# An output projection with some of its products saved, and the last residual columns turned another way

## The chip, the cores and the metric

The kernel runs on one core of one Trainium2 chip. The metric is the device time of one execution in microseconds, the median of several runs. The engines of a core that matter here are TensorE (PE, matrix products), VectorE (DVE), ScalarE (ACT), GpSimd (POOL, here mostly as an issuer of DMAs) and SyncE (SP, which issues the loads of weights). Each works through its own queue of instructions in an order that is fixed when the kernel is compiled, and waits on semaphores for the others.

## What is computed

One layer of a decoder trunk over 256 tokens with 2048 features, all in float32. Cut to what matters:

```
h = rms_norm(x, mix_norm_g);  z = h @ w_in            # one projection for all mixers
ha = mLSTM heads of z, normed and gated               # 4 heads of 256
hb = forgetting attention heads of z                  # 8 heads of 128
x = x + concat([ha, hb]) @ w_out                      # the output projection, 2048 x 2048
h = rms_norm(x, ffn_norm_g)
a, g = split(h @ w_up)                                # the up stage, 2048 x 11264
x = x + (gelu(causal_dwconv(a)) * g) @ w_down         # the down projection
x = x + sigmoid(rms_norm(x, ple_norm_g) @ w_ple_gate) * (p @ w_ple_proj)
```

## The kernel before

**Products.** A float32 product is made of three matmuls in float32r: every operand is split into a high part (a cast on ScalarE) and the rest (a subtraction on VectorE), and hi*hi, hi*lo and lo*hi are added in PSUM (`three`, lines 355 to 358; `token_group` has the same three in lines 345 to 347). The left operand, activations turned so that features lie on partitions, is kept in tiles of 128 features (a K tile): `hT` for the input projection, `catT` for the output projection, `x2T` for the up stage. A column of such a tile holds the 256 tokens' high part and then their low part. The right operand is a weight tile, loaded from HBM by SP into one of the raw buffers (512 KB for 128 x 1024), split by ScalarE and VectorE into `hi` and `lo` buffers, of which there are four of each, and used by PE. The work is a list of blocks; `run_stream` (line 261) walks through it, loads as far ahead as raw buffers are free and splits up to three blocks ahead (`AHEAD_SPLIT`). After each block it lets two steps of "side jobs" go (`pull`), generators that do the small work of the mixers. In the up stage and after it `run_units` does the same with a lead of four units and a larger set of buffers.

**The order** on each engine's queue is settled at compile time by a scheduler that takes instructions by their place in the program and by when it reckons that they are ready; so PE's order can differ from the text of the program by some matmuls. `between` and `behind` (lines 1611 to 1621) pin a hook behind the latest split.

**Seven products instead of eight.** For two K tiles and 1024 columns (two halves of 512), and two halves of 128 tokens, there are eight products of blocks. The pair can be computed in seven (Winograd's form): sums of the four blocks of the left operand are made once per pair (`sums_of`, line 453: five short VectorE operations and a cast), sums of the weight blocks for each pair and column group (`split3` and `split4`: four additions of 128x512), and four results P1, P5, P6, P7 go to PSUM banks of their own and are combined afterwards. `pair_group` (line 360) does that in the input projection for two pairs of three column groups (`FOX_ORDER`), `up_group` (line 1627) in the up stage. Strings give the order of blocks: "p" is a plain K tile (12 matmuls), "a" and "b" the four steps of the first and second pair (3, 6, 6, 6 matmuls). The plain products use four PSUM banks of one tag ("mm" or "aux"), the sums four of the other; the next group swaps the tags.

**The output projection before** (lines 980 to 1013): four column groups of 512, each `token_group` with eight blocks of two K tiles by 512 columns, so twelve matmuls a block and 384 in all. K tiles 8 to 15 (attention heads) come first, then 0 to 7, since the mLSTM heads end later; before the fifth block of the first group `pull_all` finishes the side jobs. At the end of a group `resid` adds the PSUM result to the residual `xs`, and turns the new residual columns into `x2T`. For the first three groups that goes by squares: VectorE transposes 32x32 squares (`square`), sixteen DMAs of 32 KB on POOL's queue put them in place (`move`, line 196), and seven blocks later `column` (line 207) scales and splits each K tile with one ScalarE and one VectorE operation. For the last group PE transposes the eight 128x128 pieces (`transpose_x`, line 157), and ScalarE and VectorE split them from PSUM. `sumsq` collects the sums of squares for the norm.

**The up stage before** (from line 1723): eleven column groups of 2 x 512, the order of each in `ORDERS`. The first has two pairs and begins with K tiles 4 to 9; its sums of the left operand are made after units 1 and 3. After unit 6 the whole residual (2 MB) is stored to HBM (`kept_x`, line 1057) on SP's queue, since its place is used as a buffer. The row scale `rstd2` is computed before the stage.

Of the kernel before, what the change touches and what calls it, by code (L numbers as in the profile page):

```python
# [15 lines left out]
P = 128  # L16
# [40 lines left out]
def layer_kernel(  # L57
# [297 lines left out]
    def three(o, ah, al, hi, lo, start=False, stop=False):  # L355
        pe.matmul(o, ah, hi, start=start, stop=False)  # L356
        pe.matmul(o, ah, lo, start=False, stop=False)  # L357
        pe.matmul(o, al, hi, start=False, stop=stop)  # L358

    def pair_group(w, actT, c0, n, order, tags, S_of, z_, evac, added):  # L360
# [15 lines left out]
        def plain(k):  # L376
            def fn(hi, lo):
                if k == first:
                    st.update({(t, h): bank(tags[0], f"pg{t}{h}") for t in range(NT) for h in range(2)})
                for t in range(NT):  # L380
                    for h in range(2):
                        o = st[t, h]
                        three(o[:, :n], *left(k, t), half(hi[:, 0], h), half(lo[:, 0], h), k == first, k == KD - 1)
                        if k == KD - 1:
                            evac(t, h, o)
                if k == KD - 1:
                    added()
            return Block([src(k)], fn)

        def seven(r):  # L390

# [13 lines left out]
            def fn1(hi, lo):  # L405
                sum_of(1, left(2 * r, 0), half(hi, 0), half(lo, 0))
# [5 lines left out]
            def fn2(hi, lo):  # L412
                three(st[0, 0][:, :n], *left(2 * r + 1, 0), half(hi, 0), half(lo, 0))
                three(st[0, 1][:, :n], *S(4), half(hi, 1), half(lo, 1))
# [19 lines left out]
            def fn4(hi, lo):  # L434
                sum_of(6, S(2), half(hi, 1), half(lo, 1))
                three(st[1, 0][:, :n], *left(2 * r + 1, 1), half(hi, 0), half(lo, 0))
                if r < len(sevens) - 1:
                    return
# [7 lines left out]
            one = Block([src(2 * r), src(2 * r + 1)], fn1, split=split1)  # L446
# [44 lines left out]
    with mixers:  # L491
# [438 lines left out]
        for g_, n in enumerate(FOX_HALVES):  # L930
# [11 lines left out]
            def added(c0=c0, n=n):  # L942
# [6 lines left out]
                for j in fox_jobs(c0, 2 * n):  # L949
                    j()  # L950

            blocks.extend(pair_group(w_in, lambda: hT, c0, n, FOX_ORDER, ("mm", "aux") if g_ % 2 == 0 else ("aux", "mm"),
                                     S_of, z_fox, evac_half, added))
# [26 lines left out]
        def resid(c, ssq, dst, gain):  # L980
            st = {}

            def f(t, b):
                xc = xs[:, t, c * 512 : (c + 1) * 512]
                dve.tensor_add(xc, b, xc)
# [12 lines left out]

        kcat = all_k[4:] + all_k[:4]
        x2T = {}  # L1000

        def get_x2T():
            if "t" not in x2T:
                x2T["t"] = new_aT("x2T")
# [12 lines left out]
    with tc.tile_pool(name="ffn", bufs=1) as fp:  # L1017
        x2 = x2T["t"]

        uA = new_aT("uA")  # L1020
# [17 lines left out]
        rstd2 = rstd_of(ssq2, "ffn")  # L1038
# [41 lines left out]
        def up_rows(t, n, b):  # L1080

            act.activation(EZ[:, t, n * 512 : (n + 1) * 512], b, AF.Copy, scale=rstd2[:, t : t + 1])

        def up_turn():
# [3 lines left out]
            def summed(t):  # L1088
                return lambda: dve.scalar_tensor_tensor(
                    out=EZ[:, t], in0=xs[:, 1, t * BLK : (t + 1) * BLK], scalar=rstd2[:, t : t + 1], in1=EZ[:, t],  # L1090
                    op0=ALU.mult, op1=ALU.add)
# [636 lines left out]
        for r in range(SEVENS_UP):  # L1728
            with_after(us[1 + 2 * r], between(lambda r=r: up_sums(r)))
# [59 lines left out]
```

## Time and profile before

| what | value |
| --- | --- |
| median of 3 runs | 1232.63 us (1232.27 to 1233.55) |
| span of the profiled execution, first to last instruction | 1230.1 us |
| output projection, by the starts of its first matmul and the next stage's | 341.4 to 429.6 us |
| the up stage's first group after it | to about 473 us |
| DMA traffic of the whole kernel | 277 MB, 225 GB/s in the mean |

The page does not show the execution's time outside the span by itself; the median lies 2.5 us above the span. Times inside the profile count from the span's start. A group of instructions is shown as line, engine, operation, result and sources, form, count, then busy time and mean ns of one. In the timeline a line is start, length, engine, source line and operation. The lengths of matmuls overlap: a new one begins before the last has ended, so the pace is read from the starts.

### The profile page before, as it was taken

Reading aid. Unit: us, or ns where it says so; the run is one execution under the profiler, and the core shown is the slowest. Engines: PE = TensorE matmul, PEld = TensorE weight load, DVE = VectorE, ACT = ScalarE, POOL = GpSimd, SP = SyncE. Lnnn points to the kernel's source line nnn. Section 1 sums busy time; section 2 is a strip of 40 time slices with the busy share of each in tenths; the row PEclk is TensorE's granted clock in tenths of the full one; section 3 lists DMA queues with packets and bytes.
Section 4 is the critical chain, followed back from the end, with each engine's and each line's share of the span. In section 5 each row is a group of like instructions: output and inputs, shape, how many; then the busy total and the mean of one; then the engine's idle time right before and its main releaser. Section 6 shows DMA issues by size and latency. Waiting matters only on the chain.

```text
span 1230.1 us, 16375 instructions
## 1 busy us (share of the span) xinstructions
PE 1224.3 (100%) x5593; PEld 1031.5 (84%) x5593; DVE 982.2 (80%) x1216; ACT 749.1 (61%) x1097; POOL 186.8 (15%) x347
## 2 busy tenths in 40 slices
PE   9999999999999999999999999999999999999998
PEld 7999988888888888888888888888888888888887
DVE  6788857665565689789998898898788999999773
ACT  7567545565554555766676676757657655556652
POOL 2011237243304301011101101110110000050000
PEclk9999999999999999999999999999999999999999
DMA  9566587686557786777687678756797895886670
GB/s 306 182 195 196 171 231 225 186 221 186 163 181 221 221 312 207 242 220 234 210 273 240 182 259 264 226 177 222 228 316 243 296 374 203 266 251 211 200 225 35
DMA packets 131444, 276.89 MB, mean 225 GB/s; under 512 B 14921, under 2 KB 24641, under 8 KB 131233
## 3 DMA queue, kind: packets, MB, share of 16 engines
q1 hardware_dynamic: 119456, 257.40, 66.0%
q0 software_dynamic: 11520, 18.29, 5.3%
q8 instruction: 44, 0.72, 0.2%
q14 instruction: 39, 0.32, 0.1%
q10 hardware_dynamic: 385, 0.16, 0.0%
HBM read 247.99 MB, written 8.93 MB: 209 GB/s over the span
## 4 chain that ended last, share of the span: by engine, by line
PE 99%; DMA 0%; SPq 0%; DVE 0%; ACT 0%; issue 0%; DVEq 0%
PE up L357 12%; PE up L358 11%; PE up L356 11%; PE tg L345 9%; PE tg L346 9%; PE tg L347 9%; PE pg L356 3%; PE pg L357 3%; PE pg L358 3%; PE dnP L1276 1%; PE dnP L1274 1%; PE dnP L1275 1%; PE upP L356 1%; PE upP L358 1%; PE upP L357 1%; PE gt L357 1%
## 5 line engine op out<-in xcount | busy, mean ns | idle before, releaser
L291 DVE TENSOR_TENSOR lo<-raw,hi 128x1024 fp32r<-128x1024 f32 (+3 forms) x130 | 153.3, 1181 | 107.8 <-ACT hi L289 107.4
L358 PE MATMUL up<-part,x2T 128*128 128x512 f32 x608 | 236.6, 389 | 0.0
L357 PE MATMUL up<-part,x2T 128*128 128x512 f32 x608 | 236.5, 389 | 0.0
L1224 ACT CAST part<-raw 128x1024 fp32r<-128x1024 f32 (+1 forms) x144 | 145.5, 1021 | 114.6 <-PE up L358 35.0
L289 ACT CAST hi<-raw 128x1024 fp32r<-128x1024 f32 (+3 forms) x130 | 132.3, 1017 | 123.7 <-PE tg L347 63.4
L1226 DVE TENSOR_TENSOR part<-raw,part 128x1024 fp32r<-128x1024 f32 (+1 forms) x140 | 164.4, 1182 | 26.7 <-ACT part L1224 20.8
L356 PE MATMUL up<-part,x2T 128*128 128x512 f32 x608 | 185.0, 389 | 0.0
L356 PEld LDWEIGHTS up<-part,x2T 128*128 128x128 f32 x608 | 114.2, 188 | 23.6
L358 PEld LDWEIGHTS up<-part,x2T 128*128 128x128 f32 x608 | 114.2, 188 | 23.6
L357 PEld LDWEIGHTS up<-part,x2T 128*128 128x128 f32 x608 | 114.1, 188 | 23.6
L347 PE MATMUL tg<-hi,hT 128*128 128x512 f32 x288 | 113.6, 395 | 0.0
L346 PE MATMUL tg<-lo,hT 128*128 128x512 f32 x288 | 113.2, 393 | 0.0
L345 PE MATMUL tg<-hi,hT 128*128 128x512 f32 x288 | 112.5, 397 | 0.0
L200 POOL DMA_DIRECT2D EZ<-Y x66 | 35.0, 538 | 372.8 <-issue 205.2
L1224 ACT CAST part<-u36r 128x1024 fp32r<-128x1024 f32 (+1 forms) x46 | 47.8, 1041 | 34.6 <-PE up L358 16.3
L1226 DVE TENSOR_TENSOR part<-u36r,part 128x1024 fp32r<-128x1024 f32 (+1 forms) x46 | 55.6, 1209 | 11.0 <-ACT part L1224 6.7
L347 PEld LDWEIGHTS tg<-hi,hT 128*128 128x128 f32 x288 | 54.1, 188 | 11.1
L346 PEld LDWEIGHTS tg<-lo,hT 128*128 128x128 f32 x288 | 54.1, 188 | 10.9
L345 PEld LDWEIGHTS tg<-hi,hT 128*128 128x128 f32 x288 | 53.8, 188 | 10.7
L1226 DVE TENSOR_TENSOR part<-u32r,part 128x1024 fp32r<-128x1024 f32 (+1 forms) x44 | 50.4, 1148 | 11.9 <-ACT part L1224 9.2
L1224 ACT CAST part<-u32r 128x1024 fp32r<-128x1024 f32 (+1 forms) x44 | 43.3, 990 | 21.3 <-PE up L358 9.0
L357 PE MATMUL pg<-lo,hT 128*128 128x430 f32 (+1 forms) x156 | 55.7, 357 | 0.0
(889 smaller groups left out, 2722.0 us busy)
## 6 DMA issues: line engine op xcount, KB each, us to landing
raw<-in_w_up_dram SPq DMA_DIRECT2D x78, 512.0 KB, 5.1
raw<-in_w_in_dram SPq DMA_DIRECT2D x71, 512.0 KB, 4.3
u36r<-in_w_up_dram SPq DMA_DIRECT2D x43, 512.0 KB, 5.0
raw<-in_w_down_dram SPq DMA_DIRECT2D x41, 512.0 KB, 6.2
u32r<-in_w_up_dram SPq DMA_DIRECT2D x34, 512.0 KB, 5.1
raw<-in_w_out_dram SPq DMA_DIRECT2D x32, 512.0 KB, 4.8
xs<-in_w_up_dram SPq DMA_DIRECT2D x21, 512.0 KB, 5.1
w2b<-in_w_down_dram SPq DMA_DIRECT2D x20, 512.0 KB, 5.5
```

The lines of the kernel that those rows point to most:

```text
L200: (other if other and (4 * a + b) % 3 else pool).dma_start(out=c[32 * b : 32 * b + 32, a::4], in_=y[32 * a : 32 * a + 32, :, b])
L289: act.copy(hi, raw)
L291: dve.tensor_sub(lo, raw, f32(hi))
L345: pe.matmul(o, ah, hi[:, i, :], start=first, stop=False)
L346: pe.matmul(o, ah, lo[:, i, :], start=False, stop=False)
L347: pe.matmul(o, al, hi[:, i, :], start=False, stop=last)
L356: pe.matmul(o, ah, hi, start=start, stop=False)
L357: pe.matmul(o, ah, lo, start=False, stop=False)
L358: pe.matmul(o, al, hi, start=False, stop=stop)
L1224: act.copy(r32(hi), raw)
L1226: dve.tensor_sub(r32(lo), raw, hi)
L1274: pe.matmul(o, ah, hi, start=first, stop=False)
```

## The change

The output projection becomes two column groups of 1024 through `pair_group`: the first with one pair (K tiles 8 and 9) in seven products, the second with two (8, 9 and 10, 11). `pair_group` takes the order of K tiles (`ks`) and a function that combines the four sums. Here `combined` adds them straight into the residual, as the down projection does it. The left sums are made by `out_sums` during the last group of the input projection. All residual columns go by squares, the last 1024 too: their moves start at the end of the second group, and `column` for K tiles 8 to 15 is hooked behind units 5, 5, 6, 6, 8, 8, 10 and 10 of the up stage. `ORDERS` starts with a one-pair group (K tiles 2 to 7 first, then pair 0, 1 mixed with 8 to 11, then 12 to 15), and has five groups with two pairs, as before. Four more raw buffers (`morex`, in places of `hT` that are free by then) serve the projection from its seventh block on. `x2T` and `uA` get their parts of the buffer when they are first written.

```diff
-ORDERS = ("pppppp" "apapapap" "bpbbbp",
-          *("pppppp" "apapapap" "pppp", "ppp" "apapapap" "bpbpbpb" "pp") * 4,
-          *("pppppp" "apapapap" "pppp",) * 2)
+ORDERS = (*("pppppp" "apapapap" "pppp", "ppp" "apapapap" "bpbpbpb" "pp") * 5,
+          "pppppp" "apapapap" "pppp")
+OUT_K = (8, 9, 10, 11, 12, 13, 14, 15, 0, 1, 2, 3, 4, 5, 6, 7)
+OUT_ORDERS = ("pppppp" "apapapap" "pppp", "ppp" "apapapap" "bpbpbpb" "pp")
...
-    def pair_group(w, actT, c0, n, order, tags, S_of, z_, evac, added):
+    def pair_group(w, actT, c0, n, order, tags, S_of, evac, added, combined, ks=tuple(range(KD))):
...
-                z = [v[:, :n] for v in z_]
-                act.copy(z[0], st[1][:, :n])
-                dve.tensor_add(z[1], st[6][:, :n], z[0])
-                dve.tensor_add(z[2], st[7][:, :n], z[1])
-                for i in (1, 3):
-                    dve.tensor_sub(z[i], st[5][:, :n], z[i // 2 + 1])
+                if r == len(sevens) - 1:
+                    combined(*(st[i][:, :n] for i in (1, 5, 6, 7)))
...
-        def resid(c, ssq, dst, gain):
-            st = {}
-
-            def f(t, b):
-                xc = xs[:, t, c * 512 : (c + 1) * 512]
-                dve.tensor_add(xc, b, xc)
-                if c < 3:
-                    if t == 0:
-                        st["y"] = squares("x2y")
-                    square(st["y"], t, 0, xc)
-                if t == NT - 1:
-                    if c < 3:
-                        side.append(columns(gather(st["y"], "x2z"), dst, c * 4, gain))
-                    else:
-                        for k0 in (c * 4, c * 4 + 2):
-                            transpose_x(dst(), k0, gain)
-                    sumsq(ssq, c, 512)
-            return f
...
-        for c in range(4):
-            grp = token_group(w_out, kcat, lambda: catT, c * 512, 512, resid(c, ssq2, get_x2T, g_ffn))
-            if c == 0:
-                fn = grp[4].fn
-                grp[4].fn = lambda hi, lo, fn=fn: (pull_all(), fn(hi, lo))
+        def out_sums(r):
+            if "t" not in S_o:
+                S_o["t"] = mp.tile([P, 2, 4, 256], F32R, tag="zb", name="S_o", bufs=3)
+            d = mp.tile([P, 512], F32, tag="qk", name="So_d", bufs=2).rearrange("p (k c) -> p k c", c=256)
+            f = sm.tile([P, 512], F32, tag="junk", name="So_f").rearrange("p (i c) -> p i c", i=4)
+            a = catT[:, OUT_K[2 * r] : OUT_K[2 * r] + 2, :]
+            dve.tensor_add(d, f32(a[..., 0:256]), f32(a[..., 256:512]))
+            sums_of(d, f, S_o["t"][:, r])
+
+        for r in range(2):
+            with_after(blocks[-7 + 3 * r], lambda r=r: out_sums(r))
+        at_out = len(blocks)
+        mk_place = mkT.rearrange("p k s -> p (k s)")
+        x2z = {}
+
+        def out_group(g_):
+            st = {}
+            def places(h):
+                if g_ == 0 and h == 0:
+                    return squares("x2y"), mp.tile([P, NT * 4, 128], F32, tag="col", name="x2z")
+                if g_ == 0:
+                    v = [mk_place[:, i * BLK : (i + 1) * BLK] for i in range(2)]
+                else:
+                    w = apool.tile([P, 2, BLK], F32, tag=f"aT{1 + h}", name=f"x2w{h}", bufs=2)
+                    v = [w[:, i] for i in range(2)]
+                return v[0].rearrange("p (t b c) -> p t b c", t=NT, b=4), v[1].rearrange("p (a c) -> p a c", c=P)
+
+            def evac(t, h, o):
+                c = 2 * g_ + h
+                xc = xs[:, t, c * 512 : (c + 1) * 512]
+                dve.tensor_add(xc, o, xc)
+                if t == 0:
+                    st[h] = places(h)
+                square(st[h][0], t, 0, xc)
+
+            def added():
+                for h in range(2):
+                    c = 2 * g_ + h
+                    move(*st[h])
+                    if g_ == 0:
+                        side.append(columns((st[h][1], done[0]), get_x2T, c * 4, g_ffn))
+                    else:
+                        x2z[c] = st[h][1]
+                    sumsq(ssq2, c, 512)
+
+            def combined(p1, p5, p6, p7):
+                c0 = g_ * 1024
+                x00, x01, x10, x11 = (xs[:, t, c0 + n * 512 : c0 + (n + 1) * 512] for t in range(NT) for n in range(2))
+                right = xs[:, :, c0 + 512 : c0 + 1024]
+                a = mqT.rearrange("p g a c -> p (g a c)")[:, g_ * 512 : (g_ + 1) * 512]
+                act.copy(a, p1)
+                dve.tensor_add(x00, p1, x00)
+                dve.tensor_add(a, p6, a)
+                dve.tensor_add(right, p5.unsqueeze(1).broadcast_to([P, 2, 512]), right)
+                dve.tensor_sub(x01, x01, a)
+                dve.tensor_add(a, p7, a)
+                dve.tensor_add(x10, x10, a)
+                dve.tensor_sub(x11, x11, a)
+
+            n7 = len(set(OUT_ORDERS[g_]) - {"p"})
+            ks = OUT_K if n7 == 2 else (*OUT_K[:2], *OUT_K[4:8], *OUT_K[2:4], *OUT_K[8:])
+            return pair_group(w_out, lambda: catT, g_ * 1024, 512, OUT_ORDERS[g_], (("mm", "aux"), ("aux", "mm"))[g_],
+                              lambda r: S_o["t"][:, r], evac, added, combined, ks)
+
+        for g_ in range(2):
+            grp = out_group(g_)
+            if g_ == 0:
+                fn = grp[6].fn
+                grp[6].fn = lambda hi, lo, fn=fn: (pull_all(), fn(hi, lo))
             blocks.extend(grp)
+
+        def third(i):
+            def f():
+                if ("x2", i) not in extra:
+                    extra["x2", i] = apool.tile([P, 2, BLK], F32, tag=f"aT{i}", name=f"morex{i}", bufs=2)
+                return extra["x2", i]
+            return f
+        more.update({f"n{i}{k}": (at_out + 6, len(blocks), lambda i=i, k=k: third(i)()[:, k]) for i in (1, 2) for k in range(2)})
...
-        for r in range(SEVENS_UP):
-            with_after(us[1 + 2 * r], between(lambda r=r: up_sums(r)))
+        with_after(us[3], between(lambda: r2.update(t=rstd_of(ssq2, "ffn"))))
+        for r, i in enumerate((1, 9)):
+            with_after(us[i], between(lambda r=r: up_sums(r)))
+        for k, i in zip(range(8, KD), (5, 5, 6, 6, 8, 8, 10, 10)):
+            with_after(us[i], between(lambda k=k: column(x2z[k // 4], k % 4, x2[:, k], g_ffn[:, k : k + 1])))
```

More of the change, by code (lines that the diff above doesn't have):

```diff
@@ L374, in src, with plain @@
             return wsrc(w, k, 1, c0, 2 * n)
-        def plain(k):
+        def plain(i):
+            k = ks[i]
             def fn(hi, lo):
-                if k == first:
+                if i == first:
                     st.update({(t, h): bank(tags[0], f"pg{t}{h}") for t in range(NT) for h in range(2)})
@@ L382, in fn @@
                         o = st[t, h]
-                        three(o[:, :n], *left(k, t), half(hi[:, 0], h), half(lo[:, 0], h), k == first, k == KD - 1)
-                        if k == KD - 1:
+                        three(o[:, :n], *left(k, t), half(hi[:, 0], h), half(lo[:, 0], h), i == first, i == KD - 1)
+                        if i == KD - 1:
                             evac(t, h, o)
-                if k == KD - 1:
+                if i == KD - 1:
                     added()
@@ L390, in seven @@
         def seven(r):
+            k0, k1 = ks[2 * r], ks[2 * r + 1]
             def S(i):
@@ L405, in fn1 @@
             def fn1(hi, lo):
-                sum_of(1, left(2 * r, 0), half(hi, 0), half(lo, 0))
+                sum_of(1, left(k0, 0), half(hi, 0), half(lo, 0))
             def split2(part, hi, lo):
@@ L412, in fn2 @@
             def fn2(hi, lo):
-                three(st[0, 0][:, :n], *left(2 * r + 1, 0), half(hi, 0), half(lo, 0))
+                three(st[0, 0][:, :n], *left(k1, 0), half(hi, 0), half(lo, 0))
                 three(st[0, 1][:, :n], *S(4), half(hi, 1), half(lo, 1))
@@ L950, in added, with combined @@
                     j()
+            def combined(p1, p5, p6, p7, n=n):
+                z_ = [v[:, :n] for v in z_fox]
+                act.copy(z_[0], p1)
+                dve.tensor_add(z_[1], p6, z_[0])
+                dve.tensor_add(z_[2], p7, z_[1])
+                for i in (1, 3):
+                    dve.tensor_sub(z_[i], p5, z_[i // 2 + 1])
             blocks.extend(pair_group(w_in, lambda: hT, c0, n, FOX_ORDER, ("mm", "aux") if g_ % 2 == 0 else ("aux", "mm"),
-                                     S_of, z_fox, evac_half, added))
+                                     S_of, evac_half, added, combined))
             c0 += 2 * n
```

18 lines of the change are left out of this document (8 added, 10 removed).

## The prediction

> **What bounds the kernel now.** First the totals and the chain that ended last, then the list of what TensorE (PE) waited for.
>
> ```profile
> span 1230.1 us, 16375 instructions
> PE 1224.3 (100%) x5593; PEld 1031.5 (84%) x5593; DVE 982.2 (80%) x1216; ACT 749.1 (61%) x1097; POOL 186.8 (15%) x347
> PE 99%; DMA 0%; SPq 0%; DVE 0%; ACT 0%; issue 0%; DVEq 0%
> PE warm L100 <- DVE ones L96: 1.1, 1, 1.1
> PE xT L162 <- DMA xs<-in_x_dram: 0.5, 1, 0.5
> ```
>
> The chain is PE for 99% of the span, and the last two lines are the whole list of PE's waits: 1.6 us, at the start. So the kernel is a queue of PE work, and an edit matters if it takes matmuls out or makes PE wait where it doesn't now. Busy time (389 ns each) overlaps; a matmul is priced by the distance between starts. In the timeline of PE (start, length):
>
> ```profile
> 341.40 0.39 PE L345 MATMUL tg<-hi,catT 128*128 128x512 f32 x1
> 345.48 0.39 PE L345 MATMUL tg<-hi,catT 128*128 128x512 f32 x1
> 429.58 0.39 PE L356 MATMUL up<-part,x2T 128*128 128x512 f32 x1
> 430.26 0.39 PE L356 MATMUL up<-part,x2T 128*128 128x512 f32 x1
> ```
>
> From the first row to the second are 18 matmuls in 4.08 us, from the third to the fourth 3 in 0.68: **0.2267 us** for a 128x512 product in both stages. The projection lasts from 341.40 to 429.58, 88.2 us, and the up stage follows without a hole.
>
> **What the change removes.** A pair of K tiles by 1024 columns is eight products of three matmuls, 24; in seven products it is 3 + 6 + 6 + 6 = 21. One pair in the first column group and two in the second save 9 matmuls of 384: 9 x 0.2267 = **2.04 us**. The up stage keeps its sum of pairs: before 2 + 4 x (1 + 2) + 1 + 1 = 16, after 5 x (1 + 2) + 1 = 16, so ORDERS only moves them.
>
> The eight transposes of residual columns 1536 to 2047 leave PE:
>
> ```profile
> 433.44 0.40 PE L358 MATMUL up<-part,x2T 128*128 128x512 f32 x1
> 433.67 0.60 PE L162 MATMUL xT<-ident,xs 128*128 128x128 f32 x4
> 434.58 0.60 PE L162 MATMUL xT<-ident,xs 128*128 128x128 f32 x4
> 437.08 0.39 PE L358 MATMUL up<-part,x2T 128*128 128x512 f32 x1
> ```
>
> Between the first and last row twelve matmuls start, 12 x 0.2267 = 2.72 us; the distance is 3.64. The transposes cost **0.92 us**. The sum on PE is 2.96 us, if PE doesn't wait. The Trainium skill ("TensorE: Matmul & The Clock Gate", Back-to-back issue gap) gives a sustained 131 ns for N=512 and 81 for N=128; by it the sum would be an estimated 1.83 us. These rows show 227, so the trace disagrees.
>
> **What it adds on VectorE.** The rows by form in the projection (mean ns after the comma), the first combining add of the down projection, whose code the new `combined` repeats, and a half add:
>
> ```profile
> L291 DVE TENSOR_TENSOR lo<-raw,hi 128x1024 fp32r<-128x1024 f32 x30 | 36.6, 1222 | 29.9 <-ACT hi L289 29.8
> L985 DVE TENSOR_TENSOR xs<-tg,xs 128x512 f32<-128x512 f32 x8 | 5.1, 683 | 0.0
> L194 DVE STREAM_TRANSPOSE x2y<-xs 128x512 f32<-128x512 f32 x6 | 4.0, 693 | 0.0
> L212 DVE SCALAR_TENSOR_TENSOR x2T<-x2z,vT,x2T 128x256 fp32r<-128x256 f32 x8 | 3.3, 472 | 0.0
> L1373 DVE TENSOR_TENSOR xs<-dnP,xs x2: 684/687/690, 1005.3 to 1108.3; 128x512 f32<-128x512 f32 x2
> L1375 DVE TENSOR_TENSOR xs<-dnP,xs x2: 1219/1222/1225, 1007.1 to 1112.0; 128x1024 f32<-128x1024 f32 x2
> L1671 DVE TENSOR_TENSOR raw<-raw x7: 685/687/693, 442.8 to 866.6; 128x512 f32<-128x512 f32 x7
> ```
>
> Second group, the fuller one: 12 plain splits at 1.22 (14.6), two pairs of 3.5 splits and four half adds (2 x 7.0), the combining (6 x 0.69 + 1.22 = 5.4), four adds and four squares at the end (5.5), eight columns (3.8): 43.4 us beside 186 matmuls, 42.2 us. The first, by the same rows, has 17.1 + 7.0 + 5.4 + 5.5, and what is left of the mixers: by the first two windows below, 7.46 + 6.92 less eight splits, 4.6. That is 39.6 beside 42.8. How full VectorE can be shows a two-pair group of the up stage (the third window) and the one after it:
>
> ```profile
> 341.20:350.00 8.80, 8.80 (x44) 7.35 (x43) 7.46 (x13) 6.80 (x12) 0.00 (x0) 1.00 0.57 184
> 350.00:363.50 13.50, 13.50 (x62) 11.13 (x61) 6.92 (x9) 5.27 (x5) 0.00 (x0) 1.00 0.57 181
> 600.50:642.70 42.20, 42.20 (x188) 34.95 (x187) 39.21 (x44) 30.50 (x43) 3.77 (x7) 1.00 0.74 234
> 642.70:685.50 42.80, 42.80 (x190) 35.46 (x189) 36.91 (x37) 27.47 (x38) 3.78 (x7) 1.00 0.77 237
> ```
>
> (window, length, then busy time of PE, weight loads, VectorE, ScalarE, GpSimd.) 39.2 of 42.2 without a PE wait. The new second group is 1.2 us over its own time. The splits run up to three blocks, 3 x 12 x 0.2267 = 8.2 us of PE, ahead of their products, and that lead hides it: I take **nothing**. With the lead gone it costs 1.2 us, and if VectorE can't be fuller than 39.2 of 42.2, 43.4 - 39.2 = 4.2. `out_sums` (four short subtractions and adds and a cast per pair) runs in the gate group before, beside 56% busy VectorE by the same view:
>
> ```profile
> 320.00:341.20 21.20, 21.20 (x96) 17.60 (x95) 11.82 (x21) 11.38 (x21) 9.94 (x18) 1.00 0.66 192
> ```
>
> The weights loaded stay 32 x 512 KB on SP's queue; a pair holds two raw buffers over four blocks, and four more buffers from the seventh block on make up for that, so I take nothing; POOL's queue has only the moves there. The sums of the second up pair go from unit 3 to unit 9, where the next group needs them first, and the row scale from before the stage to unit 3: both before their use, with VectorE lighter at the start of the up stage; nothing for PE.
>
> PSUM banks: a group's plain products take the banks that the previous group's sums used. After the last seven stand two plain blocks, 24 matmuls, 5.4 us, before the up stage wants them. The combining frees the last bank after four VectorE operations that read PSUM and one between, 4.0 us, with splits between them later. The down projection has the same code with as little time; there the sums' last reader came late and PE, whose order is set at compile time, had other matmuls in front:
>
> ```profile
> 1005.32 0.68 DVE L1373 TENSOR_TENSOR xs<-dnP,xs 128x512 f32<-128x512 f32 x1
> 1012.59 0.39 PE L1274 MATMUL dn(0, 0)_8868<-part,uA 128*128 128x512 f32 x1
> 1014.10 0.69 DVE L1377 TENSOR_TENSOR Y<-dnP,Y 128x512 f32<-128x512 f32 x1
> ```
>
> The next group began before the sums had all been read. I take nothing here; the bound is 2 us.
>
> **The step that can cost most: columns 8 to 15 of x2T.** Of these, 12 to 15 came through PE, transposed 5 us into the up stage, and 8 to 11 by a move that had ended before it. Now both halves come by squares, 32 DMAs of 32 KB on POOL's queue, and `column` on ScalarE and VectorE. The move of the first group today:
>
> ```profile
> 364.30 0.39 PE L345 MATMUL tg<-hi,catT 128*128 128x512 f32 x1
> 365.21 1.29 DVE L194 STREAM_TRANSPOSE x2y<-xs 128x512 f32<-128x512 f32 x2
> 367.09 4.24 POOL L200 DMA_DIRECT2D x2z<-x2y  x8 [33.08 <-ACT junk L168]
> 375.26 1.58 POOL L200 DMA_DIRECT2D x2z<-x2y  x3 [0.29 <-DMA x2z<-x2y]
> DMA to landing us min/median/max: 1.7/4.4/7.1
> L211 ACT ACTIVATE x2T<-x2z,vT x12: 494/498/509, 384.5 to 433.3; 128x256 fp32r<-128x256 f32 x12
> ```
>
> The next group starts at 364.30; POOL issues the sixteen, 0.53 us each, from 2.8 to 12.5 us after that, and the last lands at 16.9 (14.2 to 19.6 by the ends). With four banks to add and square instead of two, the first half waits for one more add and square (1.4 us), and its last bank is done three matmuls (0.7) sooner: 17.6. A `column` (0.50 + 0.47) makes it **18.6 us** (15.9 to 21.3). PE wants column 8 after six plain blocks and the first product, 75 matmuls: **17.0 us**. In order, PE would stand 1.6 us (0 to 4.3). But the order may differ from the text: above, the transposes came after matmuls of the next stage. Behind column 8 stand 18 matmuls of the pair (4.1 us) that need only columns 0 and 1. The second move issues behind the first, 9.7 us later by these rows: 28.3, against column 12 after 141 matmuls, 32.0. I take **0**, because cover and lateness are alike and the trace shows ready matmuls put first; the ends are 0 and 4.3.
>
> The Trainium skill ("DMA: Bandwidth & Descriptors", Anatomy of one DMA) fits 2.0 us plus bytes over 436 GB/s, an estimated 2.1 us for 32 KB; by it column 8 would come 2.3 us sooner and nothing would wait. The median here is 4.4, so it flatters.
>
> What crowds the place:
>
> ```profile
> 435.00:440.00 5.00, 5.00 (x24) 4.15 (x23) 4.23 (x7) 3.45 (x6) 0.00 (x0) 1.00 0.96 379
> 445.00:450.00 5.00, 5.00 (x23) 4.13 (x22) 4.49 (x8) 1.51 (x3) 0.00 (x0) 1.00 1.05 384
> ACT part L1224 <- DMA raw<-in_w_up_dram: 4.2, 2, 2.7
> 430.60 0.35 SPq L1057 DMA_DIRECT2D kept_x<-xs  x1
> ```
>
> (the last two numbers of a window are DMA share and GB/s.) The 2 MB copy of the residual and the loads of the up stage, all on SP's queue, fill the DMA engines just there, and splits already waited for a load, 2.7 us at most. Two moves add 1 MB, 2.7 us at 384 GB/s. `column` stands in the queues of ScalarE and VectorE, in order: while it waits for the landing, the splits of the next units wait behind it, and PE for those.
>
> **The sum.** 2.04 + 0.92 = 2.96 us off a span of 1230.1: 1227.1. What lies around the span, 1232.63 - 1230.1 = 2.5 us, stays: **1229.7 us** for the median.
>
> **Rivals.**
> *Columns in time only partly* (0.24): PE stands for column 8 or for a split behind it; 1.6 us, at most 4.3: 1231.3, to 1234.0. For it: 18.6 against 17.0. Against: 4.1 us of matmuls that could go ahead.
> *The wait takes over* (0.16): with the copy in flight the moves land like the slowest, 7.1 us or more; as POOL waits for landings after some ten issues, 5.3 us of issues, a landing, six more issues and a landing stand one behind another: 3.5 + 5.3 + 7.1 + 3.2 + 7.1 + 1.0 = 27.2, 10.2 late, less 4.1 covered: 6.1 us, 1235.8, slower. It decides once column 8 is more than 4.1 + 2.96 = 7.1 us late; 2.5 more make it slower by what can be told. For it: DMA at 0.96 to 1.05. Against: 7.1 was the longest of 48.
> *VectorE becomes the bound in the projection* (0.08): 1.2 to 4.2 us lost there, 1230.9 to 1233.9. For it: 43.4 us of work beside 42.2. Against: the lead, and the emptier group before it.
> *A removed matmul is worth 131 ns* (0.02): then 1230.8; the rows above show 227 everywhere.
>
> **How the numbers follow.** The forecast without a new PE wait has 0.50. A measurement of this kernel can tell about 0.2%, 2.5 us, from no change, and the forecast is only 0.5 us beyond it; so of its 0.50 some 0.05 fall to "same", and 0.02 of the partial case to faster. Faster 0.47, same 0.37, slower 0.16. Range: 2.96 is all that PE can give, and the three runs spread over 1.3 us, 0.7 each way, so 1229.0 at the bottom; at the top the partial case with its end, 1234.0. What is left out is most of the slower case.
>
> **What would show it.** Right: 9 fewer 128x512 matmuls and no L162 row at the start of the up stage, the projection 2.0 us shorter, still no PE wait after 10 us. Wrong: PE waiting on `x2T` from L212 or on a split about 17 us into the up stage (columns), on VectorE's lo parts in the second group (VectorE), or a DMA landing of x2w over 7 us.

## The result and the profile after

The changed kernel takes 1252.01 us (median of 4 runs, 1251.31 to 1252.52), the kernel before 1232.77 us (median of 4 runs on the same chip). The ratio is 1.0155, 95% interval 1.0141 to 1.0169: **slower by 19.2 us**, where 3 us less were forecast. The profiled execution took 1252.27 us.

The page of the changed kernel: totals, the clock granted to TensorE in 40 slices of the span, and the chain that ended last.

```profile
span 1250.5 us, 16418 instructions
PE 1229.9 (98%) x5576; PEld 1031.6 (82%) x5576; DVE 1008.9 (81%) x1260; ACT 757.4 (61%) x1107; POOL 196.8 (16%) x363
PEclk9999999999999979999999999999999999999999
PE 95%; DMA 2%; DVE 1%; issue 1%; SPq 0%; ACT 0%; POOL 0%; DVEq 0%; ACTq 0%; POOLq 0%
```

PE has 17 matmuls fewer, as it should: nine products and eight transposes. But the chain, 99% PE before, now runs through DMA and VectorE as well, and one slice has a lower clock. The list of what PE waited for, which before held only the first 2 us of the kernel:

```profile
PE upP L357 <- ACT part L1287: 8.6, 2, 7.7
PE up L357 <- ACT part L1287: 3.5, 2, 3.0
PE up L357 <- ACT x2T L212: 1.5, 1, 1.5
...
PE upP L358 <- DVE part L1289: 0.8, 2, 0.5
```

All the rows shown are waits of the up stage (`up`, `upP`). Where the stages begin shows the same, in PE's timeline; first after, then the one row of before that the prediction does not have:

```profile
340.96 0.39 PE L357 MATMUL pg<-hi,catT 128*128 128x512 f32 x1
427.10 0.84 PE L357 MATMUL up<-part,x2T 128*128 128x512 f32 x3
1146.24 0.39 PE L357 MATMUL gt<-part,x3T 128*128 128x512 f32 x1
```

```profile
1126.15 0.39 PE L356 MATMUL gt<-part,x3T 128*128 128x512 f32 x1
```

The projection lasts 86.14 us instead of 88.18, 2.04 less. From there to the last stage (`gt`, the gate) it is 719.14 us instead of 696.57. That is 22.57 more with 0.92 us of transposes less, so 23.5 us are lost in between, counted against a start every 0.2267 us. They lie in two places, the first up group and the last two.

**The early loss, 444 to 463 us.** Windows of 5 us (length, busy time of PE, weight loads, VectorE, ScalarE, GpSimd, then clock, DMA share, GB/s), and PE's timeline:

```profile
442.00:447.00 5.00, 2.26 (x10) 1.53 (x9) 3.17 (x6) 1.09 (x2) 1.60 (x3) 1.00 0.96 381
447.00:452.00 5.00, 0.08 (x1) 0.08 (x1) 1.74 (x2) 2.58 (x3) 2.64 (x5) 0.73 1.05 336
452.00:457.00 5.00, 3.23 (x7) 1.60 (x7) 3.05 (x5) 1.52 (x3) 4.23 (x8) 0.50 0.98 295
457.00:462.00 5.00, 5.00 (x12) 3.94 (x13) 2.36 (x5) 1.13 (x3) 4.23 (x9) 0.50 0.70 209
```

```profile
443.87 0.39 PE L359 MATMUL upP<-part,x2T 128*128 128x512 f32 x1
451.92 1.22 PE L357 MATMUL upP<-part,S_up 128*128 128x512 f32 x2 [7.66 <-ACT part L1287]
...
454.81 0.63 PE L359 MATMUL upP<-part,S_up 128*128 128x512 f32 x1
456.99 0.80 PE L357 MATMUL up<-part,x2T 128*128 128x512 f32 x1 [1.55 <-ACT x2T L212]
...
458.01 0.63 PE L357 MATMUL up<-part,x2T 128*128 128x512 f32 x1
458.43 0.63 PE L358 MATMUL up<-part,x2T 128*128 128x512 f32 x1
...
463.26 0.39 PE L357 MATMUL up<-part,S_up 128*128 128x512 f32 x1
```

PE stands for 7.7 us and again for 1.5, and in between and behind that it starts a matmul every 0.427 us instead of 0.227, at a granted clock of 0.50. From the first row to the last 22 matmuls start, which is 5.0 us of work in 19.39: **14.4 us** lost. "Busy" hides the slow clock: the last window is 5.00 of 5.00 busy with 12 matmuls instead of 22. What PE stood for, in ScalarE's queue:

```profile
442.47 0.62 ACT L458 CAST S_up<-EZ 128x512 fp32r<-128x512 f32 x1
448.03 0.58 ACT L1756 COPY xs<-upP 128x512 f32<-128x512 f32 x1 [4.95 <-DMA kept_x<-xs]
449.88 1.99 ACT L1287 CAST part<-raw 128x1024 fp32r<-128x1024 f32 x2 [1.26 <-DMA raw<-in_w_up_dram]
455.48 1.04 ACT L1287 CAST part<-raw 128x1024 fp32r<-128x1024 f32 x1 [3.61 <-PE upP L359]
456.43 1.70 ACT L212 ACTIVATE x2T<-x2w,vT 128x256 fp32r<-128x256 f32 x4
```

Three candidates stand in one queue: a copy of P1 that waits for the 2 MB store, a cast that waits for the pair's second weight tile, and behind both the moved columns. Those are late by themselves too, as VectorE's squares and POOL's issues in the timeline show, and the landings in the view of the tile:

```profile
430.60 0.70 DVE L195 STREAM_TRANSPOSE x2w<-xs 128x512 f32<-128x512 f32 x1
...
435.86 1.29 DVE L195 STREAM_TRANSPOSE x2w<-xs 128x512 f32<-128x512 f32 x2
437.14 4.23 POOL L201 DMA_DIRECT2D x2w<-x2w  x8 [26.76 <-ACT junk L169]
...
447.97 2.64 POOL L201 DMA_DIRECT2D x2w<-x2w  x5 [1.00 <-DMA x2w<-x2w]
```

```profile
DMA to landing us min/median/max: 2.6/5.4/9.0
```

The first issue comes 10.0 us after the up stage began, the sixteenth ends at 450.6, and the first column is at work on ScalarE at 456.43, **29.3 us** into the stage.

**The late loss, 23.5 - 14.4 = 9.1 us between 848 and 898 us**, in the tenth and above all the eleventh up group. The ten groups up to there have 1875 matmuls (189 for a group with one pair, 186 for one with two). Some 1.5 us are lost at 849 to 852, in the tenth group; the rest behind 885.30, by when 1951 matmuls of the stage have started, so 76 into the eleventh group, at its pair. The timeline there, rows of SP, ScalarE and PE:

```profile
878.55 7.54 SPq L201 DMA_DIRECT2D EZ<-Y  x10
886.19 0.60 SPq L1264 DMA_DIRECT2D xs<-in_w_up_dram  x1
...
890.90 1.04 ACT L1287 CAST part<-xs 128x1024 fp32r<-128x1024 f32 x1 [3.88 <-DMA xs<-in_w_up_dram]
...
892.00 1.25 PE L357 MATMUL up<-part,x2T 128*128 128x512 f32 x4 [2.95 <-ACT part L1287]
```

Ten issues of squares, the output of the tenth group, hold SP's queue for 7.5 us, the weights behind them land late, ScalarE waits for them and PE for ScalarE. But the squares alone don't make the loss. The kernel before has the same ten in the same place, some 10 us into the eleventh group, and PE does not wait there:

```profile
865.78 7.78 SPq L200 DMA_DIRECT2D EZ<-Y  x10
```

What does differ there is how far the loads have come: behind the ten issues SP has six weight tiles of the up stage left to load in the kernel before, eight here.

### The profile page after: what moved, and what is told of

It reads as the page before. It is cut to its first block, busy times and chain, and to the rows that moved or that the text cites. A ratio compares the mean times of both kernels' runs of the same rounds, so it can differ in the third digit from the quotient of the medians.

```text
span 1250.5 us, 16418 instructions
## 1 busy us (share of the span) xinstructions
PE 1229.9 (98%) x5576; PEld 1031.6 (82%) x5576; DVE 1008.9 (81%) x1260; ACT 757.4 (61%) x1107; POOL 196.8 (16%) x363
## 4 chain that ended last, share of the span: by engine, by line
PE 95%; DMA 2%; DVE 1%; issue 1%; SPq 0%; ACT 0%; POOL 0%; DVEq 0%; ACTq 0%; POOLq 0%
PE up L358 11%; PE up L357 11%; PE up L359 11%; PE tg L346 6%; PE tg L347 6%; PE tg L348 6%; PE pg L357 5%; PE pg L358 5%; PE pg L359 5%; DMA x2w<-x2w 1%; PE dnP L1338 1%; PE dnP L1337 1%; PE dnP L1339 1%; PE upP L357 1%; PE gt L358 1%; PE gt L357 1%
## 5 line engine op out<-in xcount | busy, mean ns | idle before, releaser
L292 DVE TENSOR_TENSOR lo<-raw,hi 128x1024 fp32r<-128x1024 f32 (+3 forms) x116 | 134.9, 1166 | 77.2 <-ACT hi L290 77.1
L290 ACT CAST hi<-raw 128x1024 fp32r<-128x1024 f32 (+3 forms) x116 | 116.4, 1006 | 97.4 <-PE tg L348 47.2
```

Source lines behind the costliest of these rows:

```text
L290: act.copy(hi, raw)
L292: dve.tensor_sub(lo, raw, f32(hi))
```

## The experiments

"Up loss" is the time from the first matmul of the up stage to the first of the gate in the profiled execution, less that of before (696.57 us; less 0.115 us for each transpose that is missing, more for each that is added).

| kernel | median us | ratio to before (95%) | up loss us |
| --- | --- | --- | --- |
| changed kernel | 1252.01 | 1.0155 (1.0141 to 1.0169) | 23.5 |
| e1_tail | 1245.01 | 1.0110 (1.0095 to 1.0125) | 13.8 |
| e2_pe_turn | 1243.71 | 1.0091 (1.0074 to 1.0108) | 11.3 |
| e3_both | 1232.49 | 1.0008 (0.9999 to 1.0018) | 2.2 |
| e15_pe_old | 1231.41 | 0.9987 (0.9978 to 0.9996) | 0.5 |
| e9_before_tail2 | 1244.15 | 1.0092 (1.0075 to 1.0109) | 12.6 |
| e11_pin_copy | 1244.66 | 1.0092 (1.0079 to 1.0106) | 15.8 |
| e5_no_col_wait | 1239.26, one run | - | 10.3 |
| e12_no_wait_pin | 1239.54, one run | - | 10.4 |
| e8_light_out | 1246.21, one run | - | 16.3 |
| e4_half | 1234.11 | 1.0012 (1.0003 to 1.0021) | 4.6 |
| e14_half_old | 1236.74 | 1.0031 (1.0020 to 1.0042) | 6.8 |
| e18_half_last | 1235.89 | 1.0019 (1.0010 to 1.0028) | 5.1 |

**Two losses, two parts of the change.** First the order of the up groups: those with two pairs stand in places 2, 3, 5, 7 and 9 instead of 2, 4, 6, 8 and 10.

```diff
-ORDERS = (*("pppppp" "apapapap" "pppp", "ppp" "apapapap" "bpbpbpb" "pp") * 5,
-          "pppppp" "apapapap" "pppp")
+ONE, TWO = "pppppp" "apapapap" "pppp", "ppp" "apapapap" "bpbpbpb" "pp"
+ORDERS = (ONE, TWO, TWO, ONE, TWO, ONE, TWO, ONE, TWO, ONE, ONE)
```

> Only the order of the up groups changes against the changed kernel: pairs per group 1,2,2,1,2,1,2,1,2,1,1 in place of 1,2,1,2,1,2,1,2,1,2,1, so that the tenth group has one pair again and the sum stays 16. Theory (three separate losses; the one near 850 to 896 us comes from a two-pair group where some raw buffers are gone): the loss there goes, 6.5 to 9 us, so 1243 to 1246 us, and PE still loses some 14 us between 440 and 463 us. Rival (the late loss is a consequence of the early one, or of the whole schedule): 1249 us or more.

It took 1245.01, as expected. Of the late loss 1 us is left near 899, another 1 us comes at 535, and the early loss stays. (The profile puts this kernel's first wait down to a move, "DMA x2w", but the matmul behind it reads no moved column; it starts at 454.10, as the second cast of weights on ScalarE ends, at 454.05.) Then the same with the columns of the second group back on TensorE, no squares and no moves for them:

```diff
-                    move(*st[h])
                     if g_ == 0:
+                        move(*st[h])
                         side.append(columns((st[h][1], done[0]), get_x2T, c * 4, g_ffn))
                     else:
-                        x2z[c] = st[h][1]
+                        for k0 in (c * 4, c * 4 + 2):
+                            transpose_x(get_x2T(), k0, g_ffn)
...
-        for k, i in zip(range(8, KD), (5, 5, 6, 6, 8, 8, 10, 10)):
-            with_after(us[i], between(lambda k=k: column(x2z[k // 4], k % 4, x2[:, k], g_ffn[:, k : k + 1])))
```

> As e1_tail, and residual columns 1024 to 2047 are turned by transposes on PE (16 of them, 8 more than before the change) instead of by squares and DMAs. Theory (the early loss is the wait for the moved columns, and the half clock after it): both losses go; PE has 9 matmuls fewer and 8 transposes more than before, 1232.77 - 2.04 + 0.92 = 1231.6 us, 1231 to 1233, no PE wait after 10 us. Rival (the 2 MB copy of the residual stops ScalarE and the loads whichever way the columns go): a wait of 4 us or more stays near 445 us, 1238 us or more.

1232.49, with nothing left of the early loss. The two parts, then, make the two losses. Is the late one a follower of the early one, or a cost of its own? The columns on TensorE with the changed kernel's own orders:

> The changed kernel with its own orders of the up groups, but K tiles 8 to 15 turned on TensorE: the late two-pair group alone. Theory (two losses that add): nothing is left near 444 to 463, the 9.1 us near 848 to 898 stay, as e9_before_tail2 had them on the kernel before: before plus 7 to 11, 1239.5 to 1243.5. Rival (the late loss follows from the early one, the loads running late since 444): under 3 us left, 1232 to 1235.

1243.71, a little above what was expected: nothing is lost near 444, and PE waits in the tenth and the eleventh group. The list of PE's waits in the up stage:

```profile
PE up L357 <- ACT part L1290: 5.2, 3, 2.9
...
PE upP L357 <- ACT part L1290: 0.7, 1, 0.7
```

And the other way round, the kernel before with nothing changed but a late two-pair group:

```diff
-          *("pppppp" "apapapap" "pppp", "ppp" "apapapap" "bpbpbpb" "pp") * 4,
-          *("pppppp" "apapapap" "pppp",) * 2)
+          *("pppppp" "apapapap" "pppp", "ppp" "apapapap" "bpbpbpb" "pp") * 3,
+          *("pppppp" "apapapap" "pppp",) * 2, "ppp" "apapapap" "bpbpbpb" "pp", "pppppp" "apapapap" "pppp")
```

> The kernel before, with the up groups' pairs ordered 2,1,2,1,2,1,2,1,1,2,1 (before: 2,1,2,1,2,1,2,1,2,1,1), so that its tenth group has two pairs; nothing else. Theory (a two-pair tenth group waits for raw buffers by itself): slower than before by 4 to 9 us, 1237 to 1242 us, PE waiting for splits near 850 to 900 us. Rival (that loss needs the early stall or the new projection): 1232.8 us, no PE wait.

1244.15, more than expected: 12.6 us of up loss for an edit that leaves the count of matmuls as it is. The late loss is a cost of putting two pairs in the tenth place, shown on both kernels, though most of it is paid in the group after it. Why that place is bad was not taken apart. SP has eight weight tiles left behind the ten squares in both of these kernels too, and six in e15_pe_old (below), where PE doesn't wait: with a late two-pair group the loads come to the squares two tiles behind. Four raw buffers (`v0` to `v3`) leave the pool as the tenth and the eleventh group begin, and a pair holds two buffers through four steps; which of these holds the loads up is open.

**What the early loss is made of.** e5_no_col_wait takes the wait for the moves away: K tiles 8 to 15 are filled from K tiles 0 to 7 by a ScalarE and a VectorE operation each, in the place of `column`; the kernel leaves out the true columns.

```diff
-            with_after(us[i], between(lambda k=k: column(x2z[k // 4], k % 4, x2[:, k], g_ffn[:, k : k + 1])))
+            def copied(k=k):
+                act.copy(x2[:, k, 0:256], f32(x2[:, k - 8, 0:256]))
+                dve.tensor_sub(x2[:, k, 256:512], f32(x2[:, k - 8, 0:256]), f32(x2[:, k, 0:256]))
+            with_after(us[i], between(copied))
```

> As e1_tail, but K tiles 8 to 15 of the up stage's left operand are filled from K tiles 0 to 7 in place of the moved columns; the squares and the 32 DMAs stay, and nothing reads what they move. Theory (waiting for the moved data is the loss): PE's waits between 440 and 463 us shrink below 3 us, so about 1230 to 1234 us. Rival (traffic: the copy of the residual, the moves and the loads crowd each other, and ScalarE waits for the copy): PE still waits 5 us or more for a split near 445 us, 1238 us or more.

1239.26: the theory's range is missed, and the time is the rival's, though PE waits for a copy and not for a split. No column waits for a DMA, and yet PE stands for 6.7 us. Two of the eight copies run early, at 442.0 and 443.5; those that release PE are queued on ScalarE behind the copy of P1 and the cast. ScalarE's timeline, then PE's:

```profile
450.40 1.04 ACT L1287 CAST part<-raw 128x1024 fp32r<-128x1024 f32 x1 [1.46 <-DMA raw<-in_w_up_dram]
451.35 0.71 ACT L1796 CAST x2T<-x2T 128x256 fp32r<-128x256 f32 x2
...
451.81 0.79 PE L357 MATMUL up<-part,x2T 128*128 128x512 f32 x1 [6.69 <-ACT x2T L1796]
```

So the copy of P1 was the next suspect. It can be put behind casts of later steps:

```diff
+                    if q == 0:
+                        with tc.issue_after(last["hi"]):
+                            act.copy(z_[:, 0], pb[1])
+                    else:
+                        act.copy(z_[:, 0], pb[1])
-                    act.copy(z_[:, 0], pb[1])
```

> e1_tail with the first up group's copy of P1 on ScalarE put behind some ten casts of the steps ahead, so that nothing stands behind the store. Theory (cover): the cast that stood behind the copy needs weights that land at about 451 by themselves, so the first wait of TensorE goes from 7.6 to 6.5 to 7.5 us and the time is 1243.5 to 1245.5. Rival (the copy's wait for the store is the cause): the first wait falls under 4 us, 1239 to 1241.5.

> e5_no_col_wait (K tiles 8 to 15 filled from 0 to 7) with the copy moved as in e11_pin_copy. Theory: the copies that stand for the columns are still queued on ScalarE behind a cast whose weights land at 450: TensorE still waits 5 to 6.7 us near 445, one time of 1237.5 to 1239.5. Rival (the store): the wait falls under 3 us, 1233 to 1236.

1244.66 and 1239.54: no gain over e1_tail and e5_no_col_wait. ScalarE's timeline in e11_pin_copy, in e12_no_wait_pin, and in the kernel before:

```profile
449.89 1.99 ACT L1287 CAST part<-raw 128x1024 fp32r<-128x1024 f32 x2 [6.84 <-DMA raw<-in_w_up_dram]
```

```profile
450.47 1.04 ACT L1287 CAST part<-raw 128x1024 fp32r<-128x1024 f32 x1 [6.59 <-DMA raw<-in_w_up_dram]
```

```profile
449.38 2.00 ACT L1224 CAST part<-raw 128x1024 fp32r<-128x1024 f32 x2 [1.49 <-DMA raw<-in_w_up_dram]
```

With the copy out of the way ScalarE stands just as long for the weights, and casts them 22.5 and 22.9 us into the stage; the store's wait had only been the first of two that end within 2 us of each other. A late landing is no news: in the kernel before the same cast starts 19.8 us into the stage, after a wait too, and PE doesn't stand. So the question is what PE has to do until then. In the kernel before it had the steps of K tiles 8 to 11; now these hang on work that is queued behind the cast. That can be tried by giving back only these four columns to TensorE, 12 to 15 still by squares and moves, which makes the count of before less nine matmuls:

```diff
-                    move(*st[h])
-                    if g_ == 0:
+                    if c == 2:
+                        for k0 in (8, 10):
+                            transpose_x(get_x2T(), k0, g_ffn)
+                    else:
+                        move(*st[h])
...
-        for k, i in zip(range(8, KD), (5, 5, 6, 6, 8, 8, 10, 10)):
+        for k, i in zip(range(12, KD), (8, 8, 10, 10)):
```

> K tiles 8 to 11 of the first up group turned on TensorE again, 12 to 15 by squares, pairs of K tiles as in e1_tail: the matmul and transpose count is that of before less nine matmuls. Theory (cover): the 7.7 us wait near 444 stands there because the steps of K tiles 8 to 11, which TensorE used to run while the second half of the pair's weights landed and ScalarE stood, cannot run before their moved columns come. With them on TensorE no wait over 0.5 us is left between 440 and 460 though the copy still stands for the store, columns 12 to 15 are in time, and the time is that of before less 2.0 plus the 1 to 1.6 seen late in e3_both: 1231.0 to 1232.3. Rival (ScalarE's stand for the store is enough by itself): a wait of 3 to 6 us is left there, 1236 to 1239.

PE's waits in the up stage of e4_half:

```profile
PE up L357 <- ACT part L1293: 1.7, 2, 1.0
PE upP L357 <- ACT part L1293: 0.8, 1, 0.8
```

The wait of 7.6 us is down to 1.0 us, and the slow stretch behind it to three matmuls: the rival's 3 to 6 us are gone and the cover theory holds in the main, and the columns 12 to 15, on ScalarE 32 us into the stage, were in time. But no wait over 0.5 us was to be left, and the time was missed by 2 us: 1234.11. In the trace PE loses 1.7 us near 452, 1.1 near 527 and 1.5 between 880 and 893.

**VectorE's crowd.** The squares came late because VectorE was full at the start of the up stage; with one pair less in the second projection group it has less to do.

```diff
-OUT_ORDERS = ("pppppp" "apapapap" "pppp", "ppp" "apapapap" "bpbpbpb" "pp")
+OUT_ORDERS = ("pppppp" "apapapap" "pppp",) * 2
```

> e1_tail with one pair of K tiles in seven products in the second projection group too (three matmuls more, 0.68 us; one pair's weight sums fewer on VectorE). Theory (VectorE's crowd delays the squares): GpSimd issues its first move at most 7 us after the up projection starts instead of 10, the first moved column is on ScalarE by +26 us instead of +29.3, the second wait of 2.1 us goes, the first one stays; one time of 1242 to 1244.5. Rival (the squares wait for something else): first move at +9.5 to +10.5 and 1245.5 or more.

POOL's first issue and the columns on ScalarE in e8_light_out, whose up stage begins at 428.16:

```profile
435.04 4.22 POOL L201 DMA_DIRECT2D x2w<-x2w  x8 [25.77 <-DVE x2w L195]
...
455.68 1.04 ACT L1287 CAST part<-raw 128x1024 fp32r<-128x1024 f32 x1 [3.62 <-PE upP L359]
456.63 1.70 ACT L212 ACTIVATE x2T<-x2w,vT 128x256 fp32r<-128x256 f32 x4
```

Half right: the moves begin 6.9 us into the stage instead of 10.0, so the crowd was what delayed them. But the columns come at 28.5 us as ever, because ScalarE's queue does not get to them, and 1246.21, one run, is the rival's time. Earlier moves alone buy nothing: the up loss is 16.3 us, against 13.8 in e1_tail.

**The new projection without its price.** The orders of before together with the columns on TensorE, so that only the projection's part of the change is left:

> The projection's part of the change alone: two column groups with one and two pairs, K tiles 8 to 15 of the up projection all turned on TensorE (eight transposes more than before), the up groups' orders those of before. Theory (the loss is made of the moved columns' place and of the late two-pair group, nothing else): the up projection runs without a wait that before has not, nine matmuls go and eight transposes come, before less 2.04 plus 0.92: 1231.0 to 1231.9 where before has 1232.2. Rival (the new projection itself starts the up projection with its weights later, which made the 1.4 us left in e3_both): waits of 1 to 2 us stay and the time is that of before within 0.3 us.

1231.41, ratio 0.9987 (0.9978 to 0.9996): 1.2 us less than the kernel before, about the 1.1 us expected, though near the edge of what the runs can tell (single executions of it took 1230.61 to 1234.15). And PE's list of waits is again what it was before:

```profile
PE warm L102 <- DVE ones L98: 1.1, 1, 1.1
PE xT L164 <- DMA xs<-in_x_dram: 0.3, 1, 0.3
```

Two more kernels have the squares for K tiles 12 to 15 on top of that; the second takes those tiles last (`"pppppp" "apapaa" "bbbb" "pppp"`):

> As e15_pe_old, but K tiles 12 to 15 by squares and moves: the counts of before less nine matmuls. If the moved columns were in time: 1230.2 to 1231.0. By e4_half they are not: there the last issue ended 23 us after the up projection began and the columns were on ScalarE at +32, and here TensorE wants K tile 12 some 122 matmuls in, at +27.7: a wait of 2 to 4 us near 455 and perhaps a slow clock behind it, 1232.5 to 1235.

> As e14_half_old with the first up group's two pairs ahead of K tiles 12 to 15 (no product more or less): K tile 12 is wanted 133 matmuls in, at +30.2. Theory (only the time at which the column is wanted decides): the wait of e14_half_old shrinks by 2 to 2.5 us, under 1.5 us left, 1230.5 to 1232.0. Rival (weights: the second pair's, wanted earlier than before, land late): a wait of 2 us or more for a cast of weights, 1233 or more.

1236.74, above what was expected, and 1235.89, the rival's time: both are slower than e15_pe_old. In e14_half_old PE first waits at 451 for the pair's weights, not for a column, and again for casts behind 459; in e18_half_last the rival's waits for casts of weights add up. The cast of the second weight tile starts 21.05 us into the stage in e15_pe_old (at 448.38, the stage at 427.33), where none of these columns is moved (19.80 in the kernel before), and 22.16 and 22.22 us in these two (451.17 less 429.01, 449.33 less 427.11); in them PE's work ahead of it starts its last matmul at 21.8 and 21.9. The sixteen moves run in the stretch in which the loads and the store already fill the DMA engines, so they are the likely cause of the lost 1.1 us; a run with the same moves elsewhere was not made.

## Why the prediction was wrong

**What PE saves (2.96 us): right.** The projection is 2.04 us shorter, to the hundredth, and the sum's price of 0.2267 us a matmul stands. The transposes are gone too; e15_pe_old, which has eight more of them than the kernel before, is 1.24 us faster, where nine products less eight transposes give 1.12.

**"ORDERS only moves them": the step that failed outright**, valued at nothing, worth 9.1 us in the trace, some 6 us between e1_tail and the changed kernel (each less the kernel before on its chip: 13.0 and 19.2), and 11 to 12 us against the kernel before when it is the only loss (e2_pe_turn, e9_before_tail2). It was argued from the sum of pairs. That a place has its own buffers and its own traffic was not looked up, though `until`, which takes buffers away there, stood in the listing.

**VectorE "nothing, hidden by the lead": right for PE in the projection, wrong for what comes after.** 43.4 us were counted for the second group. Windows of the changed kernel show where they went: its two projection groups and the ten us behind.

```profile
340.96:384.40 43.44, 43.44 (x198) 35.95 (x197) 33.78 (x43) 23.15 (x30) 0.00 (x0) 1.00 0.71 239
384.40:427.10 42.70, 42.70 (x190) 35.34 (x189) 37.51 (x48) 25.72 (x37) 16.91 (x32) 1.00 0.55 166
427.10:437.10 10.00, 10.00 (x46) 8.28 (x45) 10.00 (x16) 5.85 (x11) 0.00 (x0) 1.00 0.73 236
```

PE waited for none of it, but some 6 us (43.4 less 37.5) spilled into the up stage, where VectorE was busy without a break and the squares stood in line. The lead that hid the splits does not hide what has to be done after the last matmul.

**Columns 8 to 15, "I take 0": the step that failed first.** The forecast began the moves 3.5 us after the group's end (it was 10.0) and had column 8 at 18.6 us (29.3). The rival "the wait takes over" had the chain of moves and nearly the right time, 27.2; it was given 0.16. That the time came so near is partly luck, as two errors cancel: the moves began 6.5 us later than it said, and the way from the first issue to the column took 19.3 us instead of 23.7. Its price was still far too low, 6.1 us for 14.4, for three reasons. The 4.1 us of the pair's products that were to cover the wait were not there: their own weights landed later than that. So it was the other way round, K tiles 8 to 11 had been the cover for the weights (e4_half against e1_tail). The columns' work on ScalarE was queued behind that landing, so that it would have been late even without a move (e5_no_col_wait, e12_no_wait_pin); the move was about as late by itself (in e11_pin_copy the first column waits for its landing, until 456.71). And behind 8 us without a matmul came the half clock. The prediction did note that `column` stands in order in ScalarE's queue, but only as a wait for others, not as one that waits for what is ahead of it.

**PSUM banks, `out_sums`, raw buffers in the projection, the row scale: nothing, as said.** No wait on any of them is in the list. **131 ns a matmul** fell with the first row: 2.04 us for nine.

**The bounds.** 4.3 us was taken as the end of the columns' cost, and 1234.0 as the top of the range, though the slow chain was already worked out at 10.2 us late. The top was kept low by a cover that no row of the trace had been read for. Of the signs of being wrong, three came as written: PE waiting for a split 17 us into the up stage, then on `x2T` from L212, and a landing of x2w over 7 us (9.0).

## What to carry to other kernels

Before an input of a saturated engine is moved to a longer chain (VectorE, POOL, DMA, ScalarE), ask what that engine will have left to run when the next load lands: the steps that lose their input may be the ones that hid the load, and the new work may be queued behind that very load. An order of groups with the same sum is not a neutral edit; look at the buffers, the queue and the landings at each place that gets a fuller group. Take such a change apart by its parts early: here the part without either price (e15_pe_old) is worth 1.2 us, and each of the other two, kept in alone, makes the kernel over 11 us slower than before (e1_tail, e2_pe_turn).

## What was not expected of the hardware

After a wait the clock is half for a while, and a wait's price has to include that. Behind the 7.7 us wait the starts come every 0.427 us against 0.227, until 462.7. How long it lasts varies between kernels with the same two waits: in e1_tail (7.6 and 1.5 us) the pace is full from 459.5 on, right behind the second wait, and in e11_pin_copy (7.4 and 1.8) it is half until 462.6 or later; after the single wait of 7.1 us in e12_no_wait_pin it is half for 3 us. The Trainium skill ("TensorE: Matmul & The Clock Gate", Part 1: The HAM clock gate) says that the array falls to half rate after an idle window of about 3.4 us and comes back after about as long a busy one, by a window that runs free. The pace it gives for the half rate, 426.7 ns at N = 512, is that of these rows, and 3 us in e12_no_wait_pin agrees. In the changed kernel the pace is half for 5.7 us behind the second wait, more than one such window and less than two, and in e1_tail it is full right behind that wait; a window that runs free allows both, but no row here shows where it begins. Nor need the wait be unbroken: in e14_half_old four matmuls start between 452.2 and 454.2, the longest wait is 1.0 us, and the clock is half all the same from 454.3 to 457.4. Here a stretch thin of matmuls was enough. Windows of it:

```profile
452.00:454.00 2.00, 1.63 (x4) 0.67 (x4) 2.00 (x2) 1.16 (x2) 0.53 (x1) 1.00 1.06 347
454.00:456.00 2.00, 1.71 (x4) 1.42 (x5) 1.98 (x3) 0.00 (x0) 0.00 (x0) 0.54 1.05 322
456.00:458.00 2.00, 2.00 (x7) 1.52 (x7) 0.69 (x1) 0.00 (x0) 0.00 (x0) 0.61 1.03 354
```

Moves of 32 KB on POOL's queue took 5.4 us to land in the median and 9.0 at most here, against 4.4 and 7.1 for the moves of the kernel before, which lie in the projection with less traffic beside them (a DMA share of 0.67 to 0.77 there, 0.70 to 1.07 here).
